# The seam between the merge and the feed-forward of a transformer layer: first operands earlier, rows loaded two pieces ahead, weight combinations in halves, the second weight's combinations a group later

## The chip, the cores and the metric

The kernel runs on one core of one Trainium2 chip. The metric is the device time of one execution in microseconds (us). Engines are named as in the profile: PE (matrix multiplication), DVE (vector), ACT (scalar), POOL and SP, which issues the transfers between HBM and the on-chip memory.

## The reference

One layer over 2048 latent tokens of width 1024, in float32, with a context of 256 tokens. The part that the change touches is the end of the first sub-layer and the beginning of the second:

```python
x = x + g1 * branch_merge(attn_x, gm_x, ga_x, gb_x, w_br_attn[l], w_br_gm[l], w_out[l])
h2 = modulate(x, norm2_g[l], sh2, sc2)          # RMSNorm, scale, shift
x = x + g2 * sq_relu_mlp(h2, w_ff1[l], w_ff2[l])  # square(relu(h2 @ w1)) @ w2, width 4096
```

Ahead of it stand the combined input projection, attention with rotary embedding, and the gated spatial branch, which the change leaves as they are.

## The kernel before

Every float32 product is made of three matmuls: each operand is split into a high half, rounded by a cast on ACT, and a low half, the difference, taken by DVE; the matmuls are high x high, high x low and low x high. Lines 182 to 184 do this in `mm3`, lines 1587 to 1589 in `product`. A matmul of 128x128 by 128x512 is the unit of the count below.

`merge` computes the gated branches and the output projection by blocks of 512 tokens (`NB` = 4 blocks of `TT` = 4 rows of 128 tokens), each row in two halves of 512 columns, eight inner pieces of three matmuls each, so 24 matmuls a half. A finished row is stored to HBM in `x1_d`, and `stored` (L1274) takes its square sum on ACT (L1278) for the next norm. Beside the last block's output projection run the steps of `h_first`, one `next(side)` for each half row: it loads pieces of x1 back, scales them by the norm (L1406, DVE), turns them by 16 transposes on PE (L188), moves them out of PSUM with ACT (L1419), and forms the operands of the first feed-forward half.

The feed-forward uses a scheme of seven products (p = 0 to 6) of half-size blocks instead of eight. `h_first` forms sums of the four quarters of a piece kk (there are `HK` = 4 pieces) in `sums`, and splits them in `halves` (cast at L1385, difference at L1386). The tiles are called `in` (products 0 and 5), `raw`, `gx` and `hb`. On the weight's side `w1_ops` loads 1 MB of the first weight for a group (L1524), splits product 0's and 1's part (L1535, L1536) and combines and splits the others' (L1541 to L1557). `ff1` runs 16 groups (`NG`); `ff1_group` takes 7 products of 12 matmuls, copies product 0 out of its bank (L1606, the copy called u3), adds products to it on DVE (L1597), applies relu and square on ACT (L1600, L1601) and stores the seven combinations. Product 1 accumulates onto product 0's bank, so it has to wait for that copy. Beside a group run the steps of `w1_ops` for the next group and of `w2_ops` (L1560 and on), which loads 1 MB of the second weight, makes four 128x512 combinations on DVE (L1573 to L1577) and stores seven 256 KB pieces. `ff2` then multiplies by them, from pieces loaded at L1690, split at L1702 and L1703.

The order of instructions on an engine is the order in which they are written where a range is pinned: the whole of `merge` up to `self.pins.append`, and `ff2`. Elsewhere, the groups of `ff1` among them, a scheduler chooses it under the dependences and the tiles that are free. The pools that matter are `f2` with 16 tiles of 128x512, `b4` with 12, `hb` with 35, `f8` with 2, and 8 banks of PSUM.

Of the kernel before, what the change touches and what calls it, by code (L numbers as in the profile page):

```python
# [2 lines left out]

# [7 lines left out]
F32R = mybir.dt.float32r  # L11
# [7 lines left out]
P = 128  # L19
# [50 lines left out]
class Kern:  # L70
# [1176 lines left out]
    def merge(self, first, start, last, ops, w1):  # L1247
        nc = self.nc
        for _ in start:
            pass  # L1250
        self.close("mid", "base")
        self.open("early")
        self.open("late", side="right")
        for tag, shape in (("md", [TB]), ("js", [HK]), ("gt", [TB])):
            self.sb(tag, shape)
        begin = self.here()
        steps = [(b, m) for b in range(NB) for m in range(KC)]
        raws, gts, ws = {}, {}, {}
        w_out = self.load_w_out()
        mod = self.mod_part(lambda: self.sb("md", [TB]), ("sh2", "sc2"), True)  # L1260

        def load(n, tag="gt"):
            raws[n] = self.br_raw(steps[n][1])
            gts[n] = self.gate_in(*steps[n], tag)

        def cast(n, lo_eng):
            ws[n] = self.br_weights(raws.pop(n), lo_eng)

        def x_row(b, tt):
            xt = self.sb("xt", [D])  # L1270
            nc.sync.dma_start(xt, self.x_block(b)[tt * P : (tt + 1) * P, :])
            return xt

        def stored(b, tt, xt):  # L1274
            nc.sync.dma_start(self.x1_d[b][tt * P : (tt + 1) * P, :], xt)
            junk = self.sb("jk", [D], mybir.dt.bfloat16)
            col = b * TT + tt
            nc.scalar.activation(  # L1278
                junk, xt, AF.Square, accum_out=self.ss2[:, col : col + 1]
            )  # L1280

        load(0, "gx")
        load(1)
        cast(0, "dve")
        last.leave(self.sb("raw", [TB]))
        next(w_out)
        inp = first
        for b in range(NB):
            y = []
            for m in range(KC):  # L1290
                n = b * KC + m
                if n + 2 < len(steps):
# [24 lines left out]
                y.append((yh, yl))  # L1317
                if b == 0:
                    next(w_out, None)
                    if m == 2:  # L1320
                        last.sums(self.sb("raw", [TB]))
                    if m == 4:
                        last.inverse()
            inp = {}
            if b + 1 < NB:
                side = self.br_inputs(b + 1, inp)
            else:
                for _ in mod:
                    pass
                self.close("early")  # L1330
                self.open("back")
                side = self.h_first(ops, w1)
            next(side)
            xt, done = x_row(b, 0), None
            for tt in range(TT):
                tok = slice(tt * P, (tt + 1) * P)
                after = x_row(b, tt + 1) if tt + 1 < TT else None
                banks = [self.bank([512]) for _ in range(2)]

                def outer(n, ks):  # L1340
                    cs = slice(n * 512, (n + 1) * 512)
                    for k in ks:
                        self.mm3(
                            banks[n], y[k][0][:, tok], y[k][1][:, tok], self.wo[k][0][:, cs],
                            self.wo[k][1][:, cs], k == 0, k == KC - 1,
                        )

                head = KC - 1 if tt == 0 else KC
                if tt == 0:
                    for n in range(2):  # L1350
                        outer(n, range(head))
                for n in range(2):
                    cs = slice(n * 512, (n + 1) * 512)
                    ps = banks[n]
                    outer(n, range(head if tt == 0 else 0, KC))
                    if n == 0 and done:
                        stored(*done)
                        done = None
                    if b + 1 < NB or (tt, n) < (TT - 1, 1):
                        next(side, None)  # L1360
                    next(mod, None)
                    part = self.sb("jk", [512])
                    nc.vector.tensor_tensor(out=part, in0=ps, in1=self.g1b[:, cs], op=ALU.mult)
                    nc.vector.tensor_tensor(out=xt[:, cs], in0=xt[:, cs], in1=part, op=ALU.add)
                done, xt = (b, tt, xt), after
            stored(*done)
            if b + 1 < NB:
                for _ in side:
                    pass
        self.pins.append(range(begin, self.here()))  # L1370
        for _ in range(2):
            next(side)
        self.close("late")
        self.open("rest")
        return side

    def halves(self, raw, p=None, kk=None):
        nc = self.nc
# [30 lines left out]
    def x1_block(self, blk, r, kk):  # L1409
        return self.x1_scaled(self.x1_load(blk, kk), r)  # L1410

    def x1_turned(self, x, kk):
        nc, raw = self.nc, {}
        for i, j in ((0, 0), (1, 0), (1, 1), (0, 1)):
            ps = self.bank([TB])
            self.transposes(ps, [x[:, i * TT + t, j, :] for t in range(TT)])
            a = raw[i, j] = self.sb("f2", [TB])
            k = kk + j * HK
            nc.scalar.activation(  # L1419
                a, ps, AF.Identity, scale=self.G2[:, k : k + 1], bias=self.S2[:, k : k + 1]  # L1420
            )
        return raw

    def h_first(self, ops, w1):
# [3 lines left out]
        keep = {}  # L1428

        def sums(kk, raw):  # L1430
            s1, s2 = (self.sb("f2", [TB]) for _ in range(2))
            ops[0][kk] = self.halves(raw[0, 0], 0)
            tt(out=s1, in0=raw[1, 0], in1=raw[1, 1], op=add)
            tt(out=s2, in0=s1, in1=raw[0, 0], op=sub)
# [8 lines left out]
                keep[kk][1] = raw[0, 1]  # L1443
            tt(out=s4, in0=raw[0, 1], in1=s2, op=sub)

        x, raw = self.x1_load(0, 0), None
        yield
        for kk in range(HK):
            self.x1_scaled(x, r)
            if kk:  # L1450
                sums(kk - 1, raw)
            yield
            raw = self.x1_turned(x, kk)
            if kk + 1 < HK:
                x = self.x1_load(0, kk + 1)
            else:
                next(w1)
            yield
        sums(HK - 1, raw)
# [59 lines left out]
    def w1_ops(self, g, out, first=False):  # L1519
# [17 lines left out]
        out[0] = [(hr[:, k, :], lr[:, k, :]) for k in range(H)]  # L1537
        out[1] = [(hr[:, H + k, :], lr[:, H + k, :]) for k in range(H)]
        yield
        t13, t24 = self.sb("b4", [2, H, P]), self.sb("b4", [2, H, P])  # L1540
        tt(  # L1541
            out=t13, in0=raw[:, :, 1, :].rearrange("p (j k) c -> p j k c", j=2),
# [13 lines left out]
        nc.scalar.copy(h, b22)  # L1556
        tt(out=l, in0=b22, in1=f32(h), op=sub)  # L1557
        out[2] = [(h[:, k, :], l[:, k, :]) for k in range(H)]
        yield

    def w2_ops(self, s):
# [92 lines left out]
        nc.sync.dma_start(dst[2], s4)  # L1654
        yield

    def ff1(self, blk, h, extra, w=None, late=()):
        if w is None:
            w = {0: {}}
            for _ in self.w1_ops(0, w[0]):  # L1660
# [2 lines left out]
        for g in range(NG):  # L1663
# [4 lines left out]
            else:  # L1668
                raws = [self.ff2_load(blk, 0, c) for c in range(2)]
                self.ready = [self.ff2_cast(raws.pop(0))], raws  # L1670
            more = extra(g)
            for _ in self.ff1_group(blk, g, w.pop(g), h):
                next(late, None)
                next(nxt, None)
                next(more, None)
# [140 lines left out]
        self.pins.append(range(begin, self.here()))  # L1816

    def ffn(self, h, w, w1, late):
        for _ in w1:
            pass  # L1820
        next(late)
        self.ff1(0, h, self.w2_ops, w, late)
        self.g2b = self.sb("g1", [D])
        h = self.operand_lists()
        mod = self.mod_part(lambda: self.sb("f2", [TB]), ("g2",), True)
# [439 lines left out]
```

## Time and profile before

| what | us |
| --- | --- |
| median of 3 runs | 3041.65 (3038.39 to 3044.37) |
| the profiled execution's own time | 3039.84 |
| its span | 3038.1 |
| PE busy | 2957.5 |
| DVE busy | 2095.2 |
| ACT busy | 1438.3 |

The profile is of one execution. A window's row gives the busy time and the count of instructions for each engine in that stretch. A timeline's row gives start, duration, engine, line and operation, and in square brackets how long the engine idled just before and what ended the wait. A group's row gives the sum and the mean of one in ns. Tile names are those of the program without the numbers of buffers.

### The profile page before, as it was taken

To read this page: it belongs to the slowest core of one execution; us is meant where nothing else is said; L and a number is where in the kernel's file an instruction comes from. 1 tells how busy PE (TensorE), PEld (TensorE's weight loads), DVE (VectorE), ACT (ScalarE), POOL (GpSimd) and SP (SyncE) were. 2 spreads that over 40 slices of the span, in tenths; PEclk is the share of its full clock that TensorE was granted. 3 is DMA by queue.
4 is the path that set the end of the run, shared out by engine and by line. 5 is a ranking of instruction groups with operands and counts; after the bars stand their busy time and mean duration, and the time that the engine had idled before them with its cause. 6 is when DMAs were issued, how large, how long until landed. Compare 5 with 4: busy or idle time off the path is not lost.

```text
span 3038.1 us, 37873 instructions
## 1 busy us (share of the span) xinstructions
PE 2957.5 (97%) x13325; PEld 2232.8 (73%) x13325; DVE 2095.2 (69%) x3007; ACT 1438.3 (47%) x2334; POOL 657.0 (22%) x470
## 2 busy tenths in 40 slices
PE   7989999998999999999999989999999999999999
PEld 4878888875555555555888878888887888888887
DVE  4867477876788877787655588776676666654555
ACT  5645765663545454454222254444454344444442
POOL 0000000000898898886222200000000000000000
PEclk9999999999999999999999999999999999999999
DMA  8686657654111000005767558888876544448554
GB/s 292 198 267 199 206 189 223 205 182 135 47 45 43 25 19 22 15 15 163 236 208 212 176 173 312 310 299 299 264 240 222 194 152 153 149 148 285 208 206 155
DMA packets 385439, 538.59 MB, mean 177 GB/s; under 512 B 37904, under 2 KB 196800, under 8 KB 385248
## 3 DMA queue, kind: packets, MB, share of 16 engines
q1 hardware_dynamic: 372880, 515.44, 51.4%
q10 hardware_dynamic: 12368, 20.73, 1.8%
q8 instruction: 105, 1.72, 0.2%
q14 instruction: 86, 0.70, 0.1%
HBM read 371.89 MB, written 164.10 MB: 176 GB/s over the span
## 4 chain that ended last, share of the span: by engine, by line
PE 83%; DVE 6%; DMA 5%; ACT 3%; issue 2%; SPq 1%; ACTq 0%; POOL 0%; DVEq 0%; POOLq 0%
PE b L1587 14%; PE b L1589 14%; PE b L1588 14%; PE b L2156 8%; PE b L2123 5%; PE b L2142 4%; PE b L182 4%; PE b L183 4%; PE b L184 4%; PE b L2078 3%; PE a L1587 3%; PE a L1588 3%; PE a L1589 3%; PE b L188 1%; DMA f<-t_d 1%
## 5 line engine op out<-in xcount | busy, mean ns | idle before, releaser
L2089 DVE TENSOR_REDUCE ts<-b 128x1 f32<-128x512 f32 x512 | 314.7, 681 | 94.5 <-PE b L2078 94.2
L2172 POOL TENSOR_TENSOR ac<-ac,p 128x512 f32<-128x512 f32 x214 | 296.0, 1415 | 55.3 <-ACT p L2146 55.3
L1703 DVE TENSOR_TENSOR b<-b,b 128x1024 fp32r<-128x1024 f32 x170 | 200.8, 1221 | 136.5 <-ACT b L1702 136.2
L1702 ACT CAST b<-b 128x1024 fp32r<-128x1024 f32 x170 | 170.7, 1051 | 223.2 <-PE b L1589 98.8
L2146 ACT ACTIVATE p<-b 128x512 f32<-128x512 f32 x384 | 197.5, 611 | 159.4 <-PE b L2142 92.6
L1588 PE MATMUL b<-b,b 128*128 128x512 f32 x680 | 265.3, 390 | 2.8 <-DVE b L1703 2.7
L1587 PE MATMUL b<-b,b 128*128 128x512 f32 x680 | 266.1, 391 | 1.6 <-DVE f L1724 1.4
L1589 PE MATMUL b<-b,b 128*128 128x512 f32 x680 | 264.7, 389 | 0.0
L2172 POOL TENSOR_TENSOR ac<-ac,t 128x512 f32<-128x512 f32 x152 | 221.8, 1488 | 0.0
L2172 POOL TENSOR_TENSOR ac<-p,p 128x512 f32<-128x512 f32 x32 | 47.9, 1517 | 772.4 <-ACT p L2146 772.4
L2123 PE MATMUL b<-h,h 128*128 128x512 f32 x576 | 202.6, 421 | 2.2 <-DVE ts L2089 1.0
L2142 PE MATMUL b<-h,h 128*128 128x512 f32 x576 | 180.9, 396 | 0.0
L2156 PE MATMUL b<-p,h 128*64 128x512 f32 x768 | 175.3, 598 | 0.9 <-ACT p L2146 0.9
L1588 PE MATMUL b<-hb,b 128*128 128x512 f32 x446 | 173.8, 390 | 0.0
L1597 DVE TENSOR_TENSOR f<-f,b 128x512 f32<-128x512 f32 x160 | 109.2, 682 | 78.8 <-issue 45.2
L1587 PE MATMUL b<-hb,b 128*128 128x512 f32 x415 | 161.6, 389 | 0.0
L1589 PE MATMUL b<-hb,b 128*128 128x512 f32 x415 | 161.3, 389 | 0.0
L2123 PEld LDWEIGHTS b<-h,h 128*128 128x128 f32 x576 | 107.2, 190 | 63.7 <-DVE ts L2089 23.2
L1588 PEld LDWEIGHTS b<-b,b 128*128 128x128 f32 x680 | 127.6, 188 | 31.3 <-DVE b L1703 4.7
L1587 PEld LDWEIGHTS b<-b,b 128*128 128x128 f32 x680 | 127.6, 188 | 29.5 <-ACT b L1702 2.3
L1589 PEld LDWEIGHTS b<-b,b 128*128 128x128 f32 x680 | 127.7, 188 | 26.4
L1587 PE MATMUL a<-f,h 128*128 128x384 f32 (+1 forms) x320 | 119.3, 377 | 13.5 <-ACT f L634 5.9
(434 smaller groups left out, 7269.4 us busy)
## 6 DMA issues: line engine op xcount, KB each, us to landing
ao_d<-f SPq DMA_DIRECT2D x224, 256.0 KB
f<-in_w_ff SPq DMA_DIRECT2D x48, 1024.0 KB
b<-ao_d SPq DMA_DIRECT2D x85, 512.0 KB
b<-w2o_d SPq DMA_DIRECT2D x85, 512.0 KB
w2o_d<-f SPq DMA_DIRECT2D x112, 256.0 KB
f<-in_w_in SPq DMA_DIRECT2D x44, 512.0 KB
f<-x_d SPq DMA_DIRECT2D x64, 256.0 KB
hb<-ao_d SPq DMA_DIRECT2D x54, 256.0 KB
```

Of the source, the lines that this page charges most:

```text
L182: mm(ps, sh, mh, start=start, stop=False)
L1587: mm(ps, wh, hh, start=start and k == 0, stop=False, skip_group_check=True)
L1588: mm(ps, wh, hl, start=False, stop=False, skip_group_check=True)
L1589: mm(ps, wl, hh, start=False, stop=k == len(w) - 1, skip_group_check=True)
L1702: nc.scalar.copy(h, f32(l))
L1703: nc.vector.tensor_tensor(out=l, in0=f32(l), in1=f32(h), op=ALU.subtract)
L2089: nc.vector.tensor_reduce(out=self.mx[:, t, h, c : c + 1], in_=ps[h], axis=AX.X, op=ALU.max)
L2123: self.nc.tensor.matmul(self.pts[j][h], k.KA[c][self.kv][:, ks], self.qa[h], start=True, stop=False, skip_group_check=True,)
L2142: self.nc.tensor.matmul(s, k.KB[c][self.kv][:, ks], self.qb[h], start=False, stop=True, skip_group_check=True,)
L2146: self.nc.scalar.activation(pt[h], s, AF.Exp)
L2156: nc.tensor.matmul(self.o[h * HD : (h + 1) * HD, :], k.V[c][:, i, self.kv * HD : (self.kv + 1) * HD], pt[h], start=j == 0, stop=j == NKT - 1,)
L2172: nc.gpsimd.tensor_tensor(out=self.acc[e][:, h], in0=old[:, h], in1=pt[h], op=ALU.add)
```

## The change

Its parts:

1. In the last block `h_first` is advanced by one extra step, so each piece is scaled, turned and summed half a row earlier. The last piece's transposes and sums and the split of the weights of group 0 move inside `merge`'s pinned range.
2. Two pieces of x1 are loaded at the beginning, not one, and each later load is issued a piece earlier.
3. The last row's square leaves the seam: `last_rows` reloads that row in two halves during group 1 and sums them.
4. Of the last piece two quarters stay in PSUM, as does the sum s1.
5. `w1_first` makes the weight combinations of group 0 in halves, as steps of that group, where before they were made ahead of it.
6. The combinations of the second weight run a group later: group 0 has none, and group 15 has two sets.

```diff
         def stored(b, tt, xt):
             nc.sync.dma_start(self.x1_d[b][tt * P : (tt + 1) * P, :], xt)
+            if (b, tt) == (NB - 1, TT - 1):
+                return
...
                 side = self.h_first(ops, w1)
+                next(side)
             next(side)
...
-                    if b + 1 < NB or (tt, n) < (TT - 1, 1):
-                        next(side, None)
+                    next(side, None)
...
-        for _ in range(2):
-            next(side)
...
+    def last_rows(self):
+        nc = self.nc
+        for n in range(2):
+            cs = slice(n * TB, (n + 1) * TB)
+            t = self.sb("f2", [TB])
+            nc.sync.dma_start(t, self.x1_d[NB - 1][(TT - 1) * P :, cs])
+            part = self.small([1])
+            col = self.ss2[:, NB * TT - 1 : NB * TT]
+            junk = self.sb("f2", [TB])
+            nc.scalar.activation(junk, t, AF.Square, accum_out=part if n else col)
+            if n:
+                nc.vector.tensor_tensor(out=col, in0=col, in1=part, op=ALU.add)
+            yield
...
-            a = raw[i, j] = self.sb("f2", [TB])
+            a = raw[i, j] = ps if (i, j) in stay else self.sb("f2", [TB])
...
-            s1, s2 = (self.sb("f2", [TB]) for _ in range(2))
+            s1 = self.sb("f2", [TB]) if kk + 1 < HK else self.bank([TB])
+            s2 = self.sb("f2", [TB])
...
-        x, raw = self.x1_load(0, 0), None
+        xs, raw = [self.x1_load(0, kk) for kk in range(2)], None
         yield
         for kk in range(HK):
+            x = xs.pop(0)
...
-            raw = self.x1_turned(x, kk)
-            if kk + 1 < HK:
-                x = self.x1_load(0, kk + 1)
-            else:
+            raw = self.x1_turned(x, kk, ((1, 0), (0, 1)) if kk + 1 == HK else ())
+            if kk + 2 < HK:
+                xs.append(self.x1_load(0, kk + 2))
+            elif kk + 2 == HK:
                 next(w1)
...
+        if g == 0 and first:
+            yield from self.w1_first(raw, out)
+            return
...
+    def w1_first(self, raw, out):
...
+        def part(p, src, h, l):
+            nc.scalar.copy(h, src)
+            tt(l, src, f32(h))
+            out[p] = [(h[:, k, :], l[:, k, :]) for k in range(H)]
+
+        (h24, l24), (h13, l13) = parts
+        tt(t13[:, 0], b12, b11)
+        tt(t24[:, 0], b22, t13[:, 0])
+        part(5, t24[:, 0], h24[:, 0], l24[:, 0])
+        yield
+        tt(t13[:, 1], b22, b12)
+        part(6, t13[:, 1], h13[:, 1], l13[:, 1])
+        yield
+        part(4, t13[:, 0], h13[:, 0], l13[:, 0])
+        yield
+        tt(t24[:, 1], b21, t24[:, 0])
+        part(3, t24[:, 1], h24[:, 1], l24[:, 1])
+        yield
+        h, l = self.sb("f2", [H, P], F32R), self.sb("f2", [H, P], F32R)
+        part(2, b22, h, l)
         yield
...
-    def ff1(self, blk, h, extra, w=None, late=()):
+    def ff1(self, blk, h, extra, w=None, late=(), first=()):
...
+            nxt = chain(first, nxt)
+            first = ()
...
     def ffn(self, h, w, w1, late):
-        for _ in w1:
-            pass
         next(late)
-        self.ff1(0, h, self.w2_ops, w, late)
+        next(w1)
+
+        def extra(g):
+            steps = [self.w2_ops(n) for n in range(NG) if min(n + 1, NG - 1) == g]
+            return chain(*steps, self.last_rows() if g == 1 else ())
+
+        self.ff1(0, h, extra, w, late, w1)
```

The first place is ACT's queue from the last piece's evictions to the first products of group 0. Before (L1419 evictions, L1278 square, L1385 operand casts, L1535 and L1550 weight casts, L1606 the copy u3):

```order
L1419 ACTIVATE f_3666_16235<-b_16230,S_76,G_75 128x512
L1278 ACTIVATE jk_16221,ss_78<-xt_16033 128x1024
L1419 ACTIVATE f_3668_16242<-b_16237,S_76,G_75 128x512
L1385 CAST in_16255<-f_3664_16228 128x512
L1535 CAST f_3678_16267<-f_3671_16251 128x1024
L1419 ACTIVATE f_3670_16249<-b_16244,S_76,G_75 128x512
L1550 CAST b_3681_16279<-b_3680_16275 128x1024
L1385 CAST hb_16295<-f_3670_16249 128x512
L1550 CAST b_3683_16283<-b_3679_16274 128x1024
```

In the changed kernel (L1434, L1400, L1552, L1593, L1659 are the same operations; L1653 and L1654 are relu and square of product 1):

```order
L1434 ACTIVATE b_16212<-b_16212,S_76,G_75 128x512
L1400 CAST in_16247<-f_3662_16197 128x512
L1400 CAST in_16253<-f_3669_16246 128x512
L1552 CAST f_3674_16259<-f_3649_16116 128x1024
L1659 COPY f_3688_16302<-b_16288 128x512
L1400 CAST hb_16274<-b_16212 128x512
L1400 CAST hb_16304<-f_3598_15895 128x512
L1400 CAST hb_16308<-f_3621_15987 128x512
L1653 ACTIVATE f_3697_16335<-b_16288 128x512
L1654 ACTIVATE f_3697_16335<-f_3697_16335 128x512
L1593 CAST b_3682_16280<-b_3681_16279 128x512
```

The second operand cast (in_16253, product 5's) now stands ahead of the weights' cast, and the cast of product 5's weights (b_3682) behind the relu and square of product 1.

The second place is PE's queue at the end of product 0. Before (b_16299 is the bank of products 0 and 1, b_16300 that of product 5):

```order
L1589 MATMUL b_16299<-in_16255,f_3678_16267 128x512
L1587 MATMUL b_16300<-in_15960,b_3681_16279 128x512
L1588 MATMUL b_16300<-in_15961,b_3681_16279 128x512
L1589 MATMUL b_16300<-in_15960,b_3682_16280 128x512
L1587 MATMUL b_16300<-in_16073,b_3681_16279 128x512
```

In the changed kernel (b_16288 for products 0 and 1, b_16289 for product 5):

```order
L1642 MATMUL b_16288<-in_16247,f_3674_16259 128x512
L1640 MATMUL b_16288<-raw_15936,f_3674_16259 128x512
L1641 MATMUL b_16288<-raw_15937,f_3674_16259 128x512
L1642 MATMUL b_16288<-raw_15936,f_3674_16259 128x512
L1640 MATMUL b_16288<-raw_16049,f_3674_16259 128x512
L1641 MATMUL b_16288<-gx_16050,f_3674_16259 128x512
```

Product 1 now follows product 0 in its own bank, and product 5's twelve matmuls come behind it.

The third place is ACT's queue in the changed kernel where group 0 ends and group 1 begins (L1653 and L1654 are group 0's last three relu and square pairs, the second and third for sums that DVE forms; L1659 copies group 1's product 0; L1570 casts the weights of group 1's products 5 and 3, and 4 and 6):

```order
L1653 ACTIVATE f_3727_16437<-f_3727_16437 128x512
L1654 ACTIVATE f_3727_16437<-f_3727_16437 128x512
L1400 CAST hb_16411<-f_3652_16147 128x512
L1653 ACTIVATE f_3688_16302<-f_3688_16302 128x512
L1654 ACTIVATE f_3688_16302<-f_3688_16302 128x512
L1400 CAST hb_16415<-f_3669_16246 128x512
L1653 ACTIVATE f_3706_16369<-f_3706_16369 128x512
L1654 ACTIVATE f_3706_16369<-f_3706_16369 128x512
L1576 CAST f_3740_16503<-f_3728_16442 128x512
L1659 COPY f_3744_16521<-b_16507 128x512
L1570 CAST b_3736_16495<-b_3735_16491 128x1024
```

Before, the same pairs stood ahead of the copy, and in place of the last cast ahead of it stood the same cast, at L1556, while the first cast for the weights of products 5 and 3 came behind the relu of the next product; it now stands ahead of that relu.

More of the change, by code (lines that the diff above doesn't have):

```diff
@@ L2 @@
 from contextlib import ExitStack
+from itertools import chain
 import concourse.bass as bass
@@ L1410, in x1_block, with x1_turned @@
         return self.x1_scaled(self.x1_load(blk, kk), r)
-    def x1_turned(self, x, kk):
+    def x1_turned(self, x, kk, stay=()):
         nc, raw = self.nc, {}
@@ L1558, in w1_ops, with tt @@
         out[2] = [(h[:, k, :], l[:, k, :]) for k in range(H)]
+        yield
+    def w1_first(self, raw, out):
+        nc = self.nc
+        sub, H = ALU.subtract, KC // 2
+        b11, b12 = raw[:, :H, 0, :], raw[:, :H, 1, :]
+        b21, b22 = raw[:, H:, 0, :], raw[:, H:, 1, :]
+        t13, t24 = self.sb("b4", [2, H, P]), self.sb("b4", [2, H, P])
+        parts = [[self.sb("b4", [2, H, P], F32R) for _ in range(2)] for _ in range(2)]
+        def tt(o, a, b):
+            nc.vector.tensor_tensor(out=o, in0=a, in1=b, op=sub)
+        def part(p, src, h, l):
[14 more added lines that the diff above has]
+        part(3, t24[:, 1], h24[:, 1], l24[:, 1])
+        yield
+        h, l = self.sb("f2", [H, P], F32R), self.sb("f2", [H, P], F32R)
+        part(2, b22, h, l)
         yield
```

## The prediction

> **What bounds the kernel now.** I began with the page's busy shares and its slices of granted clock, went on to a table of windows around the seam between merge and feed-forward, then to the timeline of that seam, and last to the end of the first ff1, whose extra work the change moves.
>
> ```profile
> span 3038.1 us, 37873 instructions
> PE 2957.5 (97%) x13325; PEld 2232.8 (73%) x13325; DVE 2095.2 (69%) x3007; ACT 1438.3 (47%) x2334; POOL 657.0 (22%) x470
> ```
>
> PE is the bound of the whole: a stage can give at most what PE loses in it. In the windows below the columns are start:end, length, busy us (instructions) of PE, PEld, DVE, ACT, POOL, then PE's granted clock, DMA share, GB/s.
>
> ```profile
> 1750.00:1800.00 50.00, 41.76 (x189) 33.46 (x188) 37.71 (x52) 25.09 (x41) 0.00 (x0) 0.91 0.39 128
> 1780.30:1786.40 6.10, 1.63 (x5) 0.75 (x4) 3.47 (x4) 3.54 (x6) 0.00 (x0) 0.82 0.72 258
> 1784.22:1791.05 6.83, 5.74 (x14) 4.04 (x13) 5.65 (x8) 3.92 (x6) 0.00 (x0) 0.50 0.58 222
> 1786.40:1798.00 11.60, 8.00 (x23) 5.45 (x22) 10.31 (x17) 7.55 (x12) 0.00 (x0) 0.79 0.23 78
> 1791.05:1797.88 6.83, 3.35 (x12) 1.87 (x11) 6.72 (x11) 3.51 (x7) 0.00 (x0) 1.00 0.06 14
> 1797.88:1801.29 3.41, 3.11 (x7) 2.49 (x8) 3.39 (x7) 3.36 (x7) 0.00 (x0) 0.50 0.86 280
> 1798.00:1813.00 15.00, 14.82 (x59) 12.11 (x60) 14.32 (x22) 9.08 (x16) 0.00 (x0) 0.89 0.75 251
> 1813.00:1825.00 12.00, 12.00 (x54) 9.86 (x53) 12.00 (x19) 6.42 (x11) 0.00 (x0) 1.00 0.72 248
> 1825.00:1850.00 25.00, 25.00 (x111) 20.43 (x110) 20.47 (x28) 13.40 (x20) 0.00 (x0) 1.00 0.92 318
> ```
>
> At full clock PE starts a matmul every 25.00/111 = 0.225 us. Two things are to be seen: PE idles only before 1798.2, and DVE is nearly full from 1786.4 to 1825 (10.31 of 11.60, 14.32 of 15, 12.00 of 12). Between 1780.3 and 1825 DVE rests for 2.63 + 1.29 + 0.68 + 0 = 4.6 us in all.
>
> ```profile
> 1778.60 1.91 PE L188 MATMUL b<-ident,f 128*128 128x128 f32 x16
> 1779.24 1.45 ACT L1419 ACTIVATE f<-b,S,G 128x512 f32<-128x512 f32 x2 [5.56 <-PE b L188]
> 1780.58 1.05 ACT L1278 ACTIVATE jk<-xt 128x1024 bf16<-128x1024 f32 x1
> 1782.28 0.61 ACT L1385 CAST in<-f 128x512 fp32r<-128x512 f32 x1
> 1782.79 1.05 ACT L1535 CAST f<-f 128x1024 fp32r<-128x1024 f32 x1
> 1783.89 0.54 PE L1587 MATMUL b<-in,f 128*128 128x512 f32 x1 [3.38 <-ACT f L1535]
> 1784.67 1.22 DVE L1536 TENSOR_TENSOR f<-f,f 128x1024 fp32r<-128x1024 f32 x1
> 1785.95 0.79 PE L1589 MATMUL b<-in,f 128*128 128x512 f32 x1 [1.09 <-DVE f L1536]
> 1795.55 0.50 PE L1587 MATMUL b<-in,b 128*128 128x512 f32 x1 [2.62 <-ACT in L1385]
> 1796.90 0.51 PE L1588 MATMUL b<-in,b 128*128 128x512 f32 x1 [0.85 <-DVE in L1386]
> 1797.54 0.58 ACT L1606 COPY f<-b 128x512 f32<-128x512 f32 x1 [0.92 <-DVE hb L1386]
> 1798.18 0.80 PE L1587 MATMUL b<-raw,f 128*128 128x512 f32 x1 [0.30 <-ACT f L1606]
> ```
>
> The gaps in square brackets sum to 3.38 + 1.09 + 2.62 + 0.85 + 0.30 = 8.24 us. In the two windows at a clock of 0.50, PE was busy 5.74 + 3.11 us and did half of that in work, so 4.4 us more are gone. **The seam loses 12.7 us now**; that is all the change can win there.
>
> **The change part by part.** *First operands sooner.* The last piece's 16 transposes (1.91 us) go ahead of the last 24 output-projection matmuls (24 x 0.225 = 5.4 us), which now cover the chain from them to product 0; the square of the last row (1.05 us) leaves that chain. Count from the end of the transposes. ACT's third and fourth evictions end about 1.5 later (two took 1.45). Then comes the cast (0.61), DVE's low half, s1 and s2. For DVE's spacing these rows serve:
>
> ```profile
> 1797.97 3.81 DVE L1386 TENSOR_TENSOR hb<-f,hb 128x512 fp32r<-128x512 f32 x6
> L1551 DVE TENSOR_TENSOR b<-b,b 128x1024 fp32r<-128x1024 f32 x23 | 28.1, 1223 | 9.4 <-ACT b L1550 7.6 <-PE b L1588 1.8
> L1601 ACT ACTIVATE f<-f 128x512 f32<-128x512 f32 x40 | 25.3, 632 | 1.1
> ```
>
> Six 128x512 operations in 3.81 us give about 0.6 each behind one another (0.7 where one needs the last), and a 128x1024 takes 1.22. So s2 is ready at 1.5 + 0.6 + 0.6 + 0.7 + 0.7 = 4.1, its cast at 4.8, the weights' high half (1.05) at 5.9 or 6: a gap of 0.6 after the 5.4. The weights' low half on DVE stands behind three more 128x512 and ends at 4.8 + 3 x 0.6 + 1.2 + wakes = 8.0; the third matmul waits some 1.5 for it. So 2.1 of the old 4.47 remain. The old 2.62 + 0.85 (product 5 waiting for the last piece's operand) go.
>
> *What is late next.* In the new order on PE, product 1 comes right after product 0 in the same bank, so the copy of the bank (0.58 and a wake of about 0.3) stands bare: **0.85**, where 0.30 showed. Product 5 comes after product 1, and ACT has the relu and square of product 1 ahead of the cast of product 5's weights: 0.63 + 0.63 + 0.61 and wakes, 2.1, and 0.3 for the low half: **2.4**. This is a wait that the change adds. Behind that cast stand the operand casts of products 6, 4, 3 and 2, and behind those DVE's low halves.
>
> *DVE's queue.* The halves of the weight combinations cost about the same DVE time as before: nine 128x512 at 0.6 are 5.4, against four such and two of 1.22, 4.8. No DVE work disappears. DVE's idle time was 4.6, to which come 1.9 in the merge after the earlier transposes (the row of 1778.60 moved); so DVE cannot reach 1825's state more than 6.5 us sooner, whatever PE does. PE, without its old losses, would want 12.7. I count DVE from the end of product 0's first wait to the last sum of group 0 that ACT needs before it can copy group 1's product 0: 35 operations of 0.6, one of 1.2 and about 1 of waits are 23.2 us. With PE's end of the output projection as zero, DVE enters this stretch at 6.3 and leaves it at 29.5; a relu, a square and the copy bring 31.2. PE, from product 5's start at 10.6, has some 72 matmuls until it needs that copy, 16.2 us, and four short waits for low halves, 1.4 together: it is there at 28.3 or 28.7. **2.5 us of stall in group 1** follow, then 1.3 and 0.6 for the weights of group 1's product 5, whose casts stand behind the copy. In group 2 product 1 again comes right after product 0, so the copy is bare (0.85), and a square of the reloaded last row, some 0.8 with its reading out, stands on ACT ahead of it: 1.6 (bounds 0 and 2).
>
> Sum for the changed seam: 2.1 + 0.85 + 2.4 + 1.4 + 4.4 + 1.6 = 12.8. A half-clock window costs 3.41/2 = 1.7 when PE has work and nothing when it waits for DVE anyway; three of the stalls may bring one each. I take half of one, 0.85 (bounds 0 and 5.1). So 13.6 against 12.7: **the seam is 0.9 us slower**, the lead of some 6 us that PE has in group 0 being given back in groups 1 and 2.
>
> *Pieces loaded two ahead* takes away DVE's 2.0 us wait for the first; DVE has room in the merge (37.71 of 50) and PE does not wait there: nothing. *The reloads* of the last row are 0.5 MB in a stretch at 248 to 318 GB/s: nothing, bounds 0 to 1.6.
>
> *The combinations of the second weight a group later.* Group 15 now has two sets: 1 MB more in, 1.75 MB more out, four more 128x512 on DVE near its end.
>
> ```profile
> 2088.00:2107.00 19.00, 18.77 (x83) 15.09 (x81) 9.68 (x15) 6.92 (x10) 0.00 (x0) 1.00 0.60 212
> 2107.00:2120.00 13.00, 12.29 (x53) 9.98 (x54) 8.11 (x10) 5.24 (x6) 0.00 (x0) 1.00 1.02 373
> 2104.23 1.99 ACT L1702 CAST b<-b 128x1024 fp32r<-128x1024 f32 x2
> 2105.30 2.36 DVE L1703 TENSOR_TENSOR b<-b,b 128x1024 fp32r<-128x1024 f32 x2 [0.25 <-ACT b L1702]
> 2107.71 0.50 PE L1588 MATMUL b<-b,b 128*128 128x512 f32 x1 [0.94 <-DVE b L1703]
> ```
>
> PE waits 0.94 for the split of ff2's first pieces. DVE gets 4 x 0.6 = 2.4 just ahead of that split, and SP the stores ahead of the next loads, at a place where the queues go to 1.02 of their share. At 373 GB/s, 2.75 MB are 7.4 us; the 19 us before have 0.40 of their share free, 7.6 us. So between 0 and +5; I take **+2.5**.
>
> In all +0.9 + 2.5 = +3.4 on the profiled execution's 3039.84 (span 3038.1). The median of before lies 1.8 above that execution, so I put +3.4 on the median: **3045.0 us**.
>
> **A rule weighed.** The row of 1791.05 shows PE busy 3.35 of 6.83, with no gap over 2.62, and the next window at 0.50. The Trainium skill, "TensorE: Matmul & The Clock Gate", section "Why this matters for your kernels", asks for no idle gap over about 3 us, else the clock halves. By that rule none of the changed seam's stalls (2.5 at most) would slow PE, and the sum would be 0.85 lower; the row speaks against it, since two gaps of 2.62 and 0.85 sufficed.
>
> **The rivals.**
> - *The gain comes through.* If DVE and ACT keep up, only 2.1 + 0.85 + 2.4 stay, 5.4 of 12.7, and group 15's extra is covered: 3041.65 - 7.3 = 3034.4. For it: DVE has 4.5 us to spare in every 25 after 1825, and the short casts may be ordered luckily. Against: DVE's 12.00 of 12.
> - *Half-clock windows decide, on the slower side.* If each of the stalls at product 0, product 5 and group 1 leaves a 3.41 us stretch less than about half busy, as the row of 1791.05 was, three windows follow: 12.8 + 5.1 - 12.7 + 2.5 = +7.7, so 3049.4; it decides once PE waits over 1.7 in such a stretch. For it: both old stalls did so. Against: part of it falls where DVE binds.
> - *The change shifts the wait and no more.* Seam 12.7 as before, group 15's extra hidden in the free 0.40: 3041.65. For it: the seam's loss is set by DVE's queue both times.
>
> **How the numbers follow.** A difference under 0.2% (6.1 us) can't be told from none here: faster is under 3035.6, slower over 3047.7. My forecast 3045.0 has 0.35, the mere shift 0.13, both within 0.2%; the gain coming through 0.24 (faster); half-clock windows 0.28 (slower). So 0.24, 0.48, 0.28. The range takes in both ends, down to 3033 for the gain with its terms a little smaller and up to 3052 with 2.5 more for the end of ff1.
>
> **What would show it.** Right: product 0 starts about 0.6 us after the last output matmul; a gap near 2.4 in front of product 5, waiting for a cast; a gap over 1.5 before group 1's product 1, waiting for ACT's copy; DVE without a rest from 1787 to 1813; more than 0.94 before ff2. Wrong: PE without gaps from product 0 on and 1800:1825 holding 111 matmuls (the gain), or two and more windows at 0.50 with PE busy in them (the slower side); a loss elsewhere, in the merge or in ff2, would make all of these wrong.

## The result, and the profile after

The changed kernel takes 3046.33 us (median of 19 runs, 3041.87 to 3053.16), the kernel before, run beside it, 3041.44 (19 runs). The ratio is 1.0017, with a 95% interval of 1.001 to 1.0023: 0.17% longer, some 5 us, which is under the 0.2% named as the bound and well within the range given. The prediction said 3045.0. The profiled execution of the changed kernel took 3046.08.

First the page's head, then the rows of the timeline of PE where it had idled at the seam (in brackets the idle time and what ended it).

```profile
span 3044.3 us, 37886 instructions
PE 2957.7 (97%) x13325; PEld 2229.0 (73%) x13325; DVE 2097.2 (69%) x3011; ACT 1439.2 (47%) x2338; POOL 656.3 (22%) x470
```

```profile
1780.36 0.51 PE L1640 MATMUL b<-in,f 128*128 128x512 f32 x1 [0.57 <-ACT f L1552]
1782.40 0.50 PE L1642 MATMUL b<-in,f 128*128 128x512 f32 x1 [1.30 <-DVE f L1553]
1785.68 0.50 PE L1640 MATMUL b<-raw,f 128*128 128x512 f32 x1 [0.72 <-ACT f L1659]
1790.57 0.50 PE L1640 MATMUL b<-in,b 128*128 128x512 f32 x1 [1.86 <-ACT b L1593]
1806.14 0.50 PE L1642 MATMUL b<-in,b 128*128 128x512 f32 x1 [0.17 <-DVE b L1553]
1812.06 0.51 PE L1640 MATMUL b<-raw,b 128*128 128x512 f32 x1 [2.20 <-ACT f L1659]
1813.89 0.79 PE L1640 MATMUL b<-in,b 128*128 128x512 f32 x1 [1.09 <-ACT b L1570]
```

PE's busy time is the same as before, and the gaps are other gaps: 3.38 + 1.09 before product 0 have become 0.57 + 1.30, the 2.62 + 0.85 are gone, and in their place stand 0.72, 1.86, 2.20 and 1.09, each where PE waits for a copy or a cast. With 0.17 at 1806.14 and a last one of 0.49 at 1840.84 they make 8.4 us, where 8.24 stood. Windows show the stretches at half clock and how full DVE is (columns as in the prediction).

```profile
1792.40:1795.80 3.40, 3.40 (x10) 2.69 (x9) 3.16 (x7) 2.45 (x5) 0.00 (x0) 0.51 1.04 379
1798.00:1813.00 15.00, 12.42 (x51) 8.93 (x49) 14.57 (x23) 8.68 (x17) 0.00 (x0) 0.99 0.47 159
1812.80:1819.63 6.83, 5.74 (x14) 4.34 (x15) 5.19 (x5) 2.93 (x3) 0.00 (x0) 0.50 0.60 192
2113.30:2116.60 3.30, 3.30 (x9) 2.61 (x8) 0.00 (x0) 0.92 (x1) 0.00 (x0) 0.51 0.96 330
```

Half of PE's 3.40 + 5.74 us there is 4.6 us, where 4.4 were lost before. So, counted as in the prediction, **the seam loses 8.4 + 4.6 = 13.0 us, where it lost 12.7**. Product 0's third matmul starts 3.5 us sooner (1782.40, where it was 1785.95), 0.7 of it because PE arrived that much sooner, and what was won there and after it is given back by 1820.

A second count does not rest on gaps. PE's arrival is the end of its last work ahead of product 0 (1780.51 before, 1779.79 now). The 400th matmul behind it starts here, in the kernel before and in the changed one (timeline):

```profile
1885.40 0.39 PE L1588 MATMUL b<-hb,b 128*128 128x512 f32 x1
1886.12 0.39 PE L1640 MATMUL b<-hb,b 128*128 128x512 f32 x1
```

That is 104.9 us behind the arrival before, and 106.3 now: by this count the seam is 1.4 us slower. A record missing in a trace moves such a count by 0.2. The two counts differ because PE loses more at a gap than its bracket says: around the 2.20 the starts lie 2.59 apart (1809.47 and 1812.06), 2.36 more than the 0.23 of full pace, and there are eight gaps in place of five.

Most of what is longer lies behind the seam. At the end of ff1 (timeline; L1626 to L1630 are the second weight's combinations, L1758 the low half of ff2's first pieces):

```profile
2105.78 0.69 DVE L1626 TENSOR_TENSOR f<-f 128x512 f32<-128x512 f32 x1
2106.98 0.68 DVE L1627 TENSOR_TENSOR f<-f,f 128x512 f32<-128x512 f32 x1
2109.04 0.69 DVE L1629 TENSOR_TENSOR f<-f 128x512 f32<-128x512 f32 x1
2109.64 0.69 DVE L1630 TENSOR_TENSOR f<-f,f 128x512 f32<-128x512 f32 x1
2110.24 2.35 DVE L1758 TENSOR_TENSOR b<-b,b 128x1024 fp32r<-128x1024 f32 x2
2110.33 0.50 PE L1640 MATMUL b<-b,b 128*128 128x512 f32 x1 [0.41 <-ACT b L1757]
2112.65 0.50 PE L1641 MATMUL b<-b,b 128*128 128x512 f32 x1 [1.82 <-DVE b L1758]
```

The four operations of group 15's second set stand among the last sums, two of them directly ahead of the split that PE waits for. 0.41 + 1.82 and half of a slow stretch of 3.3 us are 3.9, against one gap of 0.94: **2.9 us more**. And in groups 9 and 12, where nothing was foreseen, PE waits for a sum on DVE. The rows of group 9:

```profile
1961.33 1.05 ACT L1552 CAST b<-f 128x1024 fp32r<-128x1024 f32 x1 [2.85 <-DMA f<-in_w_ff]
1962.41 1.22 DVE L1553 TENSOR_TENSOR b<-f,b 128x1024 fp32r<-128x1024 f32 x1 [3.00 <-ACT b L1552]
1966.02 0.50 PE L1640 MATMUL b<-hb,f 128*128 128x512 f32 x1 [0.69 <-DVE f L1650]
```

The next group's first weight lands late, ACT waits 2.85 us for it, DVE waits 3.00 behind ACT with the sums queued behind that, and PE 0.69; in group 12 it is 1.08. Together 1.8 us in the brackets. From the 400th to the 1300th matmul the changed kernel takes 2.5 us more. So in these two traces the stretch behind the arrival is 1.4 + 2.5 + 2.9 = 6.8 us longer, the arrival is 0.7 earlier, and the spans differ by 6.2. The medians differ by 4.9: two single executions give the places of the loss, and its size only roughly.

### The profile page after: what moved, and what is told of

It is laid out like the page before. It is cut to its first block, busy times and chain, and to the rows that moved or that the text cites. A ratio compares the mean times of both kernels' runs of the same rounds, so it can differ in the third digit from the quotient of the medians.

```text
span 3044.3 us, 37886 instructions
## 1 busy us (share of the span) xinstructions
PE 2957.7 (97%) x13325; PEld 2229.0 (73%) x13325; DVE 2097.2 (69%) x3011; ACT 1439.2 (47%) x2338; POOL 656.3 (22%) x470
## 5 line engine op out<-in xcount | busy, mean ns | idle before, releaser
L1758 DVE TENSOR_TENSOR b<-b,b 128x1024 fp32r<-128x1024 f32 x170 | 200.7, 1220 | 137.5 <-ACT b L1757 136.7
```

Source lines behind the costliest of these rows:

```text
L1758: nc.vector.tensor_tensor(out=l, in0=f32(l), in1=f32(h), op=ALU.subtract)
```

## The experiments

The theory going in: in the seam the queue of splits on DVE (and ACT) sets the pace, so the time of groups 0 and 1 hardly depends on how early PE starts; some 3 of the 5 us are lost at the end of ff1. The rivals: PE's order and its bare copies make the loss, or the shift is free. Ratios below are to the kernel before, run on the same chip; the changed kernel's is 1.0017.

Total times also hold what varies ahead of the seam: the kernels of the sixth and the eighth experiment are the same up to group 1, and PE reaches product 0 at 1781.5 in one trace and at 1787.2 in the other. So this table counts from PE's arrival to the start of the 400th matmul behind it (the seam) and of the 1400th (behind the end of ff1), with the time at a granted clock of 0.50 up to the 400th. Each row is one execution, in us.

| kernel | to the 400th | of it at half clock | to the 1400th |
| --- | --- | --- | --- |
| before | 104.9 | 10.2 | 334.5 |
| changed | 106.3 | 10.2 | 341.4 |
| 1, two sets in the middle | 104.4 | 3.4 | 335.3 |
| 2, shift alone | 105.3 | 13.6 | 338.7 |
| 3, product 5 first | 104.1 | 6.8 | 338.7 |
| 4, low halves on POOL | 105.7 | 10.2 | 340.7 |
| 5, low halves left out | 100.5 | 6.8 | 333.3 |
| 6, first and third | 103.1 | 3.4 | 333.0 |
| 7, one piece ahead | 110.7 | 13.6 | 344.0 |
| 8, sixth, row in group 4 | 103.8 | 6.8 | 335.6 |
| 9, weights' split first | 104.4 | 6.8 | 339.2 |
| 10, sixth and ninth | 103.5 | 10.2 | 334.3 |
| 11, tenth, two groups later | 101.9 | 6.8 | 331.7 |
| 12, tenth, row in group 4 | 101.5 | 3.4 | 333.4 |

The slow stretches come in pieces of 3.4 us, and their number changes from trace to trace. The program of the first experiment is that of the changed kernel up to group 7, with gaps in the seam alike within 0.3 us; yet 6.8 us less of it run at half clock, and its seam is 1.9 us shorter.

**1. The two sets in the middle.**

```diff
-            steps = [self.w2_ops(n) for n in range(NG) if min(n + 1, NG - 1) == g]
+            steps = [self.w2_ops(n) for n in range(NG) if n + (n < 8) == g]
```

> The changed kernel, but group 8 and not group 15 takes two sets of the second weight's combinations (groups 9 to 15 take their own). Theory: the end of the first ff1 costs 3.0 of the change's 4.9 us (gaps of 0.41 and 1.82 and a 3.4 us stretch at half clock, against one gap of 0.94 before), because the second set lands on DVE just ahead of ff2's first split: the time falls by 3.0, to about 3043.3, with one gap of about 0.9 ahead of ff2 and no slow stretch there. Rival, the loss is in the seam itself: no change, 3046.3. If late loads of the first weight in groups 9 and 12 (gaps of 0.69 and 1.08) come from the shift, they go too for the groups after 8 and it falls by 4 to 5.

Measured: 3042.51 us, ratio 1.0002 (0.9993 to 1.0011). The end of ff1 reads as it did before, with no slow stretch behind it (timeline):

```profile
2109.63 0.50 PE L1641 MATMUL b<-b,b 128*128 128x512 f32 x1 [0.94 <-DVE b L1758]
```

3.8 us less, with the seam's gaps as in the changed kernel. One gap of 0.34 is left in the later groups. The rival, that the loss is in the seam and the time stays, is out. From the 1300th to the 1400th matmul this trace takes 24.5 us, the changed kernel's 27.1 and that of before 24.2. Part of its gain over the changed kernel's trace is the shorter seam of the table, which the edit did not make.

**2. The shift alone, in the kernel before.**

```diff
-        self.ff1(0, h, self.w2_ops, w, late)
+        def extra(g):
+            return chain(*[self.w2_ops(n) for n in range(NG) if min(n + 1, NG - 1) == g])
+
+        self.ff1(0, h, extra, w, late)
```

> The kernel before with one part of the change alone: the second weight's combinations a group later, two sets in group 15. Theory: +3.0 us at the end of ff1 (3044.4), the seam's gaps as before but for a little relief of DVE in group 0; with gaps in later groups from late loads of the first weight, up to +4.8 (3046.2). Rival, the shift is free since the queues have room: 3041.4.

Measured: 3044.63 us, ratio 1.0009 (1.0001 to 1.0018), with the changed kernel's two gaps at the end of ff1 (timeline):

```profile
2109.08 0.50 PE L1588 MATMUL b<-b,b 128*128 128x512 f32 x1 [0.41 <-ACT b L1703]
2111.39 0.50 PE L1589 MATMUL b<-b,b 128*128 128x512 f32 x1 [1.81 <-DVE b L1704]
```

A gap of 0.48 in group 9 came too. The seam is that of before within 0.4 us, and from the 1300th to the 1400th matmul it takes 26.9, 2.7 us more than before. With the first experiment: the shift costs about 3 us both where it is added and where it is taken away.

**3. Product 5 ahead of product 1 in group 0.**

```diff
-        if g or blk:
-            u2 = fifth()
-            yield
+        u2 = fifth()
+        yield
...
-        if not g and not blk:
-            u2 = fifth()
-            yield
```

> The changed kernel with product 5 written ahead of product 1 in group 0 as in all other groups. Theory, that DVE's and ACT's queue of splits sets the pace: the waits of 0.72 and 1.86 before products 1 and 5 shrink by about 1, the stall of group 1 (2.20 and 1.10) grows by about as much or stays, in all 0 to -1.8 us (3044.5 to 3046.3). Rival, that the order on PE eats the gain: both waits go and nothing comes in their place, -2.6 or with the slow stretch after them -4.3 (3042 to 3043.7).

Measured: 3043.59 us, ratio 1.0009 (0.9999 to 1.0019), 2.7 us less than the changed kernel by the medians, more than the theory gave. Its gaps (timeline):

```profile
1787.26 0.50 PE L1640 MATMUL b<-raw,f 128*128 128x512 f32 x1 [0.72 <-ACT f L1659]
1790.93 0.50 PE L1640 MATMUL b<-in,b 128*128 128x512 f32 x1 [0.63 <-ACT b L1593]
1812.86 0.50 PE L1640 MATMUL b<-in,b 128*128 128x512 f32 x1 [2.75 <-ACT b L1570]
```

The wait for product 5's cast shrinks from 1.86 to 0.63, that of group 1 becomes one of 2.75 in place of 2.20 and 1.09. The rival's picture, both waits gone and nothing in their place, did not come either: the copy stays bare, and a stall of group 1 stays. By the times alone the order of the two products is not shown to be worth anything, since this interval and the changed kernel's overlap. In the table the seam is 2.3 us shorter, with one slow stretch of 3.4 us less.

**4. Seven low halves on POOL.**

```diff
+                    eng = self.nc.gpsimd if (p, kk) in ((4, 1), (4, 2), (3, 1), (3, 2), (3, 3), (2, 1), (2, 3)) else None
-                    ops[p][kk] = self.halves(keep[kk][p], p, kk)
+                    ops[p][kk] = self.halves(keep[kk][p], p, kk, eng)
```

> The changed kernel with seven of the 128x512 low halves (pieces 1 and 2 of product 4, 1 to 3 of product 3, 1 and 3 of product 2) taken by POOL, which is idle there. Theory, DVE's queue is what group 1 waits for: 7 x 0.6 = 4.2 us leave that queue, so the stalls of 2.20 and 1.10 in group 1 and the slow stretch behind them (1.7) go: -4 to -5 us (3041.3 to 3042.3), PE's ff1 groups from 2 on that much earlier. Rival, the bare copies and ACT's order hold PE: no change, 3046.3. Rival, POOL and DVE slow each other: slower than the changed kernel, and the DVE operations beside it longer than 0.69.

Measured: 3045.47 us, ratio 1.0016 (1.0007 to 1.0025): nothing gained. Groups by form between 1799.5 and 1809, while POOL works (behind the shapes the count, then busy us and mean ns, then idle us before them):

```profile
L1401 DVE TENSOR_TENSOR hb<-f,hb 128x512 fp32r<-128x512 f32 x3 | 4.7, 1568 | 0.0
L1591 DVE TENSOR_TENSOR b<-b,b 128x512 fp32r<-128x512 f32 x1 | 1.8, 1753 | 0.0
L1651 DVE TENSOR_TENSOR f<-f,b 128x512 f32<-128x512 f32 x2 | 1.3, 674 | 0.0
```

The same groups in the changed kernel, with POOL idle:

```profile
L1401 DVE TENSOR_TENSOR hb<-f,hb 128x512 fp32r<-128x512 f32 x7 | 4.8, 684 | 0.0
L1650 DVE TENSOR_TENSOR f<-f,b 128x512 f32<-128x512 f32 x3 | 2.1, 684 | 0.4 <-PE b L1642 0.4
```

The third rival: beside POOL, DVE's operation on two operands in SBUF takes 1568 ns, not 684. The sums whose second operand is a bank of PSUM (L1651) stay at 674. The Trainium skill, "GPSIMD Engine Reference", section "1. Specifications", says that the two engines share their interface to SBUF and that it is contended by DVE instructions with two SBUF inputs; the trace agrees, 1568 against 674. So this run took hardly any work out of DVE's time and says nothing for or against the theory. Hence the next.

**5. The same seven left out.** The edit is the last one's, with `if eng: return h, h` in `halves`. The kernel leaves out seven differences and takes high x high twice in their place, so it does not compute the layer, and only its time is of use.

> The changed kernel with the same seven low halves left out altogether (the high half is used in their place, so those products are computed less finely), which takes 4.2 us out of DVE's queue without giving it to POOL. Theory, DVE's queue is what group 1 waits for: its stalls of 2.20 and 1.10 and the slow stretch behind them go, -4 to -5 us against the changed kernel (about 3041.5), and the copy of group 2's product 0 comes some 5 us earlier. Rival, the order on PE and ACT holds PE and DVE's length does not matter: no change, 3046.3, with the stall of 2.2 in its place.

Measured: 3039.13 us, ratio 0.9987 (0.9978 to 0.9996). The window of group 0's end and the start of group 1:

```profile
1798.00:1813.00 15.00, 14.95 (x65) 11.94 (x65) 14.81 (x22) 11.97 (x20) 0.00 (x0) 1.00 0.51 177
```

PE is busy 14.95 of 15 us at full clock, where it was 12.42, and it does not idle in group 1 at all; DVE is as full as before, with other work. 0.30% or 9 us against the changed kernel is twice what was expected; the traces differ by 8.1 up to the 1400th matmul. Besides the stalls of 2.20, 1.09, 0.17 and 0.49 the slow stretch of 6.83 and the late loads of groups 9 and 12 are gone (4.0 + 2.9 + 1.8 = 8.7), and a slow stretch of 3.4 us at 1783.4 is new (1.7). The seam itself is 5.8 us shorter, where 4 to 5 were expected. What DVE has to do is what group 1 waits for. The waits of group 0 at products 1 and 5 are still there (0.72 and 1.85): these hang on the order on PE and ACT, as the third experiment shows.

**6. Both edits that helped.** The edits of the first and third together.

> Group 8 takes the two sets, and product 5 stands ahead of product 1 in group 0: both edits that helped. If they are independent, 3046.3 - 3.8 - 2.7 = 3039.8, about 1.6 under the kernel before. If the gain of the second came from DVE's queue in later groups by chance, no better than the first alone, 3042.5.

Measured: 3040.88 us, ratio 0.9992 (0.9983 to 1.0001), 2.5 us under the kernel before by the medians. Two gains that add up would give 1.0017 - 0.0015 - 0.0008 = 0.9994, so this agrees, though its interval overlaps that of the first experiment alone. In the table its seam is 1.3 us shorter than the first's, with 3.4 us at half clock in both.

**7. Pieces loaded one ahead.**

```diff
-        xs, raw = [self.x1_load(0, kk) for kk in range(2)], None
+        xs, raw = [self.x1_load(0, 0)], None
...
-            if kk + 2 < HK:
-                xs.append(self.x1_load(0, kk + 2))
-            elif kk + 2 == HK:
+            if kk + 1 < HK:
+                xs.append(self.x1_load(0, kk + 1))
+            if kk + 2 == HK:
                 next(w1)
```

> The changed kernel with its pieces of x1 loaded one ahead, as before the change. The prediction costed the second piece ahead at nothing. If that holds the time stays, 3046.3. Rival: with every step a half row sooner a load has one half-row step (about 5.5 us) less to land, and DVE, which works in order, holds up the merge's own evictions and PE: gaps in the merge and 8 to 12 us longer, 3055 to 3058.

Measured: 3058.6 us, ratio 1.0054 (1.0038 to 1.007). The waits between 1750 and 1797 (us in total, times, longest):

```profile
DVE f L1421 <- DMA f<-x_d: 11.8, 2, 6.3
PE b L189 <- DVE f L1421: 4.0, 2, 3.6
PE b L1640 <- ACT f L1552: 3.9, 1, 3.9
```

The rival is right. In the changed kernel DVE does not wait for a piece at all in the same place. The second piece ahead is what makes the earlier steps possible.

**8. The last row's square in group 4.** The sixth kernel with `if g == 4` in place of `if g == 1`.

> As the kernel with both edits, and the last row is reloaded and squared in group 4, not in group 1 with its second square falling in group 2. Theory: the square ahead of the copy is what group 2 waited 0.49 for; without it -0.5 us against the kernel with both edits, gap in group 2 gone. Rival, that wait is for the copy alone: no change.

Measured: 3040.62 us, ratio 0.9997 (0.9988 to 1.0006). The gap of 0.49 is not in its group 2, but it is not in the sixth kernel's either, and nothing can be told from the times. The trace says what the gap is. One of 0.52 now stands in group 5, where the second square has gone (timeline):

```profile
1903.20 0.63 ACT L1387 ACTIVATE f<-f 128x512 f32<-128x512 f32 x1 [4.27 <-DMA f<-x_d]
1903.83 0.57 ACT L1659 COPY f<-b 128x512 f32<-128x512 f32 x1
1904.44 0.50 PE L1640 MATMUL b<-raw,b 128*128 128x512 f32 x1 [0.52 <-ACT f L1659]
```

ACT waits for the reloaded half row, squares it, and only then takes the copy that product 1 needs. In the changed kernel's group 2 the same three stand in a row, with a wait of 1.69 for the reload; in the sixth's the square starts at 1838.86 without a wait, and no gap follows. So the gap belongs to a reload that lands late, as the theory has it in part; that its place is worth time is not shown.

**9. The weights' split ahead of the last sums.**

```diff
-        sums(HK - 1, raw)
         next(w1)
+        sums(HK - 1, raw)
```

> The changed kernel with the high and low half of product 0's weights taken ahead of the last piece's sums, so that product 0 has both when PE comes: the gaps of 0.58 and 1.30 go. Theory, the splits behind them on ACT and DVE set the pace: product 5 waits longer (1.86 grows to 2.2 or more), the stall of group 1 stays at its absolute time, and 1.9 us of gap removed bring no more than 0 to -0.5 in all (3045.8 to 3046.3). Rival, PE's own gaps are the loss: -1.9, 3044.4.

Measured: 3042.86 us, ratio 1.0004 (0.9995 to 1.0013). The gaps of 0.57 and 1.30 are gone, product 5's is unchanged, and the stall of group 1 is there (timeline):

```profile
1791.58 0.50 PE L1640 MATMUL b<-in,b 128*128 128x512 f32 x1 [1.86 <-ACT b L1593]
1814.13 0.50 PE L1640 MATMUL b<-raw,b 128*128 128x512 f32 x1 [2.17 <-ACT f L1659]
```

The expectation failed: it was to bring 0 to 0.5 us, and in the trace 2.0 stay at the 400th matmul and 2.2 at the 1400th; the time fell by 0.13%. The matmul behind group 1's stall starts 31.1 us after the last output matmul has left PE (1814.13 - 1783.05), in the changed kernel 32.3 (1812.06 - 1779.79). DVE's waits between 1778 and 1814 show from where, in the changed kernel first:

```profile
DVE hb L1401 <- ACT hb L1400: 1.9, 1, 1.9
DVE b L1590 <- ACT b L1593: 0.7, 1, 0.7
```

and in this one:

```profile
DVE f L1553 <- ACT f L1552: 3.1, 1, 3.1
DVE hb L1401 <- ACT hb L1400: 1.1, 2, 0.7
```

The 1.22 us operation at L1553 went to an earlier place, and DVE's rest of 1.9 right before its long full stretch shrank to 0.7. A queue that sets the pace is shortened by filling a hole ahead of it, which the expectation overlooked. That is 1.2 of the 2.0; the rest goes with the slow stretch behind the stall, 3.4 us in this trace and 6.8 in the changed kernel's.

**10 to 12. Towards a faster kernel.** The tenth is the sixth with the edit of the ninth. The eleventh has `n + (n < 10) + (n < 7) == g` besides, two groups' delay at the beginning. The twelfth is the tenth with the last row in group 4.

> Group 8 with two sets, product 5 ahead of product 1, and the weights' split ahead of the last sums. Here product 5's wait ends later than DVE's backlog starts, so about 1 of the 1.7 us of gaps at product 0 should remain as gain against the kernel with the first two edits: about -1, 2.5 + 1 under the kernel before (ratio near 0.9988). Rival: all given back, ratio as that kernel's, 0.9992.

> As the last, with the combinations of the second weight two groups later from the beginning (groups 0 and 1 none, groups 8 and 10 two sets), which takes 2.4 us of DVE out of group 1's time. Theory: DVE's queue behind the stall of group 1 is shorter, less for groups 2 and 3 to make up: 0 to -2 us against the last. Rival, the second double group lets late loads of the first weight stall PE: +1 or more.

> Group 8 with two sets, product 5 ahead of product 1, the weights' split ahead of the last sums, and the last row's square in group 4. Theory: as e10 less what the square costs in group 2, so ratio 0.9988 to 0.9993 against the kernel before, with its interval's upper end near 1. Rival: the row's place gives nothing, 0.9993.

Measured: 3039.3 us, ratio 0.9993 (0.9984 to 1.0002); 3037.75 us, ratio 0.9993 (0.9984 to 1.0001); 3040.27 us, ratio 0.9996 (0.9987 to 1.0005). None can be told from the sixth, and each interval reaches 1. In the table their seams take 103.5, 101.9 and 101.5 us, with 10.2, 6.8 and 3.4 at half clock, where the sixth takes 103.1 with 3.4: with as much at half clock, the twelfth is 1.6 shorter, and in the tenth's trace the clock takes that back. All five kernels with two sets in the middle and product 5 first lie between 0.9992 and 0.9997, so about 0.06% under the kernel before is likely and not shown for any one of them; all are faster than the changed kernel. In the tenth and twelfth the gaps at product 0 are gone, and the wait for product 5's weights has grown from 0.6 to 1.4, as expected; a stall of 2.75 stands in group 1 in each of the sixth to the twelfth with product 5 first. The two groups' delay did not take it away, so it is not the combinations of the second weight that it waits for. In the eleventh's trace DVE works without rest from 1801.2 to 1809.6 on low halves, sums and the next group's combinations, and the cast that PE waits for follows.

## Why the prediction was right

Point by point, by its own steps:

- **The start of product 0** was to keep 0.6 + 1.5 us of gaps: 0.57 + 1.30.
- **The bare copy** was put at 0.85 and **product 5's wait** behind relu and square at 2.4: 0.72 and 1.86.
- **Group 1's stall** by the two counts, DVE's and PE's, was 2.5, with 1.3 and 0.6 behind it: 2.20, and 1.09. DVE's last sum ahead of the copy ends 29.9 us after PE's arrival, where 29.5 was worked out, and DVE is busy for 24.62 of the 26 us from 1787 to 1813. Experiment 5 shows that this queue is the cause.
- **Group 2's stall** was mis-sized: 1.6, and 0.49 measured. I had product 1 come right after product 0 there; in the trace product 5 and nine matmuls more lie between, so the copy is not bare, and PE waits only because the reload ahead of the square lands late. The four short waits, 1.4, were nearly absent (0.17).
- **Half clock** was mis-sized the other way: half of one window, 0.85, and it was 4.6 in a stretch of 3.4 and one of 6.83 us, within the bounds. I argued that a slow clock costs nothing while PE waits for DVE; but PE had work for 9.1 of these 10.2 us. Gaps of 0.72 and 1.86 preceded the first; the second began between the gaps of 2.20 and 1.09. By the rule of the Trainium skill, "TensorE: Matmul & The Clock Gate", section "Why this matters for your kernels", gaps under some 3 us leave the clock alone; the runs differ, and the row of before was the better guide. The stalls came to 8.4 in place of 12.8, the clock to 4.6 in place of 0.85, so that 13.6 for the seam was 13.0. That these errors cancel is luck, the more so as the first experiment's trace, with the same order, has a third as much at half clock. The seam is 0.3 us slower by this count and 1.4 by the 400th matmul, where 0.9 was forecast; in the first experiment's trace, with the same order, it is 0.5 shorter than before. So one trace does not settle the sign.
- **The combinations a group later** were to cost 2.5, between 0 and 5: 2.9 in the trace, and experiments 1 and 2 give 3.8 and 3.2 by the medians, 2.6 and 2.7 by the traces from the 1300th to the 1400th matmul.
- **Two pieces ahead** were costed at nothing, and in neither trace does PE idle in the merge's last 80 us; but what it would cost to go without was not worked out, and it is about 11 us (1.0054 against 1.0017). The earlier steps depend on it.
- **Not foreseen**: the waits behind late loads in groups 9 and 12, 1.8 us in the brackets. Their cause stays open. Such gaps are there with the shift alone as well (0.48), and shrink or go where the sets meet in the middle; but experiments 5 and 7 keep the shift to the end and have none. A late load does not make one by itself: before, ACT waits up to 3.3 us for the first weight in the groups of ff1, and in the sixth experiment up to 6.4, without a gap on PE.
- Of the rivals, the gain coming through did not occur, since DVE did not keep up. The half-clock rival's picture did come: 10.2 us at 0.50 are its three windows, with PE busy in them, which the prediction named as a sign that it is wrong. The time stayed below that rival's 3049.4 because the stalls were 4.4 us smaller than it took them.

## What to carry to other kernels

Ahead of moving work earlier for the engine that binds the whole, count the queue of the engines that feed it up to the point where both meet again; a lead that they can't follow is given back there, and a hole in their queue that can be filled is worth looking for. Compare traces from a common mark such as the arrival at a product: the totals of single executions also hold what varies elsewhere, and the slow stretches of the clock differ between traces of one order. A task that is moved one step later over a loop piles up at the loop's last step, so let it meet the schedule in the middle, where it cost nothing that could be measured. A load that is costed at nothing may be what makes another step possible: price the case without it.

## What the runs showed of the hardware

- POOL is not free relief for DVE: seven 128x512 operations took 1.8 us each on POOL (12.5 us of busy time), beside which DVE's operations on two SBUF operands went from 684 to 1568 ns, while those with one operand in PSUM stayed at 674. In the trace of before, 30 operations of the same shape on POOL between 1600 and 1760 took 1294 ns each.
- PE's clock was at half for 3.4 us behind idle gaps of 0.72 and 1.86 us that ended 4.9 us apart, and for 6.8 us from 1812.80 on, between the end of a gap of 2.20 (1812.06) and that of one of 1.09 (1813.89).
- The same gaps can leave the clock alone or not: behind 0.33 or 0.34 and 1.32 or 1.33 us at product 0, a stretch of 3.4 us at half clock followed in experiments 3, 4, 5 and 8, and none in 1 and 6.
